# A hybrid attention and delta-rule backbone on one core: the order planner of TensorE puts dense products between small matmuls

## The chip, the cores and the metric

The kernel runs on one core of a Trainium2 chip. The metric is the device time of one execution in microseconds (us). PE is TensorE's matmul part, PEld its weight load, DVE VectorE, ACT ScalarE, POOL GpSimd and SP the engine whose queue issues the DMA transfers.

## What is computed

Two layers over 512 latent tokens and 256 context tokens of width 1024, all in f32. Each layer projects the modulated, normalised tokens once, and splits the columns into three kinds of heads: gated DeltaNet in both directions (8 heads of 64), global attention (4 query heads, 2 key heads) and windowed attention (the same, with a sink). An output projection and an MLP with squared ReLU follow. Cut to what matters:

```python
def hybrid_layer(x, cx, ...):
    sh_a, sc_a, gt_a, sh_m, sc_m, gt_m = ada_mod(cond, w_mod, b_mod)
    ...
    a_qkv, a_z, a_beta, a_alpha, b_qkv, c_qkv = split_cols(modulate(x, g_attn, sh_a, sc_a) @ w_in)
    ...
    o_a, oc_a = gdn_mixer(...)          
    o_b, oc_b = global_gqa(q, k, v, qc, kc, vc)
    o_c, oc_c = window_gqa(q, k, v, qc, kc, vc, wa_sink)
    x = x + gt_a * (jnp.concatenate([o_a, o_b, o_c], axis=-1) @ w_out)
    x = x + gt_m * sq_relu_mlp(modulate(x, g_mlp, sh_m, sc_m), w_mlp_in, w_mlp_out)
```

The delta rule (`gated_delta_chunked`) runs in chunks of 64 tokens: a triangular system per chunk and head, and then a scan over the chunks, whose state goes from one chunk to the next. Context chunks come first, then latent ones.

## The kernel before

The kernel doesn't write its instructions in the order of the code. `Model.run` (line 1744) records every operation of both layers in a `Program` through `Program.add` (line 353): its engine, what it must wait for, a modelled duration (`cost`, line 389), and for PE a number `dense`: the share of the 128 rows of the array that the product uses, times 0.6 if its output has at most 64 columns (line 382). Then `Program.layout` (line 428) plans the whole kernel in one pass of a list scheduler and `issue` (line 639) writes the instructions out engine by engine in the planned order. On the chip each engine works through its own order and waits where an operand isn't there. All instructions are issued by line 683, so the profile names that line throughout, and groups are told apart by tile names.

Dense products (`dense` 1.0) are those of the projections and the MLP (`ps<-b,w`, `ps<-w,b`, `ps<-h,w`; each weight slice is loaded into `st` and split into two tiles `w`, high and low part, by ACT and DVE, and three products per tile pair make up an f32 product), attention's scores, transposes and value products (`ps<-a,a`, `ps<-r,a`, `ps<-cst,g`, `ps<-g,g` of 128 rows), and the modulation `ps<-sm,cs`, which streams the 512 KB slices of `w_mod` through two buffers `sm`. Small products are those of the delta rule: the key products (`key_products`, line 1443, 64 rows), the inverse of the triangular systems (`pre`, line 1530, 32 rows, tiles `s`) and the scan (`scan_step`, line 1629, 64 rows and 64 columns, tiles `u`, `v`, `kv`, `kaq`, results in `pu`). A scan step has three groups of products on its chain (`pw`, `px`, `pk`), 8 heads and directions each, with work of DVE or ACT between them, and one off the chain (`po`). In the trace one f32 product counts twice, so a group of 8 stands there as x16.

What sets the order: an operation's rank is the length of the longest chain of modelled work from it to the end (line 445). For every engine there is a heap `avail` of the operations whose inputs are there, best rank first. At each step the engine whose clock is earliest takes the top of its heap; if its tiles have no free slot it is parked, otherwise it is placed. PSUM has 5 slots `ps` and 3 slots `pu` (`KINDS`, line 36).

The planner also models TensorE's clock with constants of its own (`WINDOW`, `COLD`, `WARM`, lines 308 to 310): it adds up the planned PE time of a stretch weighted by `dense` (`work`), and sets a flag `warm` for the next stretch from the sum. While the flag is off, a matmul is planned to take twice its time. In the kernel before, this model changes only planned durations; the choice among ready products goes by rank alone.

The order of the program is: modulation of layer 0; input projections for the first half of the delta-rule heads, its key products, systems and scan; the second half; attention's projections; attention and scan together with the modulation of the next stages; output projection and MLP; and the same for layer 1, whose context output isn't needed.

Of the kernel before, what the change touches and what calls it, by code (L numbers as in the profile page):

```python
# [303 lines left out]
PE, ACT, DVE, POOL, SP = range(5)  # L304
# [3 lines left out]
WINDOW = 4096 / 1.2  # L308
COLD = 0.36
WARM = 0.66  # L310
TABLES = {AF.Exp: 0, AF.Tanh: 0, AF.Ln: 1}


class Program:
# [38 lines left out]
    def add(self, eng, name, args, kw):  # L353
# [30 lines left out]
        if eng == ACT:  # L384
            op.table = TABLES.get(args[2])
        self.ops.append(op)
# [41 lines left out]
    def layout(self):  # L428
        ops = self.ops
# [10 lines left out]
        for k, l in chains.items():  # L440
            n = KINDS[k][2] + KINDS[k][3] + max(KINDS[k][5:])
# [43 lines left out]
        clock, avail, future = [0.0] * 5, [[] for _ in range(5)], [[] for _ in range(5)]  # L485
        parked = {k: [] for k in KINDS}
        queues, front, order, table = 0.0, 0, [], 0
        warm, work, spill, window = False, 0.0, 0.0, 0
# [44 lines left out]
        while len(order) < len(ops):  # L533
            best = None
            for e in range(5):
                t = clock[e] if avail[e] else max(clock[e], future[e][0][0]) if future[e] else None
                if t is not None and (best is None or t < best[0]):
                    best = t, e
            if best is None and early:
                n = heapq.heappop(early)[1]  # L540
# [5 lines left out]
            t, e = best  # L546
            now = max(now, t)
            while future[e] and future[e][0][0] <= t:
                n = heapq.heappop(future[e])[1]
                heapq.heappush(avail[e], (-ops[n].rank, n))  # L550
            n = heapq.heappop(avail[e])[1]
            o = ops[n]
            if longest - o.rank > AHEAD[e] and n != front and n not in forced and any(
                    x.slot is None and x.kind in HOARD for x in o.tiles):
# [25 lines left out]
            if e == PE:  # L580

                w = int(t / WINDOW)
                while window < w:
                    warm = work > (COLD if warm else WARM) * WINDOW
                    work, window = spill, window + 1
# [3 lines left out]
                d = (end - t) * o.dense  # L589
                over = min(1.0, max(0.0, end - (w + 1) * WINDOW) / (end - t))  # L590
                work, spill = work + d * (1 - over), spill + d * over
# [36 lines left out]
            while early and (longest + early[0][0] <= AHEAD[ops[early[0][1]].eng] or early[0][1] == front):  # L628
                n = heapq.heappop(early)[1]
# [1192 lines left out]
```

## Time and profile before

| | |
|---|---|
| median of 3 runs | 2344.86 us (2334.07, 2344.86, 2356.42) |
| profiled execution | 2335.23 us |
| its span, first to last instruction | 2333.4 us |
| mean granted clock of TensorE | 0.929 |
| busy: PE, PEld, DVE, ACT, POOL | 2119.1, 1690.0, 1214.4, 878.4, 358.0 us |
| matmuls | 18584 |

The span is cut into 40 slices of 58 us in the page's second part; a digit is a busy share in tenths, and PEclk is the clock granted to TensorE in tenths of full speed. The stages are read from the names of the tiles in each stretch: 0 to 200 us the first modulation and projections, 200 to 709 the mixers of layer 0, 709 to 1340 its output projection and MLP, 1340 to 1909 projections and mixers of layer 1, 1909 to the end its output projection and MLP.

### The profile page before, as it was taken

To read this page: it belongs to the slowest core of one execution; us is meant where nothing else is said; L and a number is where in the kernel's file an instruction comes from. 1 tells how busy PE (TensorE), PEld (TensorE's weight loads), DVE (VectorE), ACT (ScalarE), POOL (GpSimd) and SP (SyncE) were. 2 spreads that over 40 slices of the span, in tenths; PEclk is the share of its full clock that TensorE was granted. 3 is DMA by queue.
4 is the path that set the end of the run, shared out by engine and by line. 5 is a ranking of instruction groups with operands and counts; after the bars stand their busy time and mean duration, and the time that the engine had idled before them with its cause. 6 is when DMAs were issued, how large, how long until landed. Compare 5 with 4: busy or idle time off the path is not lost.

```text
span 2333.4 us, 45381 instructions
## 1 busy us (share of the span) xinstructions
PE 2119.1 (91%) x18584; PEld 1690.0 (72%) x18584; DVE 1214.4 (52%) x2481; ACT 878.4 (38%) x1717; POOL 358.0 (15%) x392
## 2 busy tenths in 40 slices
PE   5899999679989899999999888989869988999999
PEld 2687788446657788888888767678636766878777
DVE  4668547765653632332333485757754655334333
ACT  4736325336432521312222363543425444222321
POOL 0133323432320000000000012244411310000000
PEclk9888899779998999999999997979769989999999
DMA  7267425894763121221221327466675532322322
GB/s 276 83 183 201 118 77 160 250 296 123 213 214 115 46 73 57 77 72 46 73 66 66 95 78 195 130 186 200 204 207 160 165 97 69 102 91 99 100 91 82
DMA packets 250224, 305.49 MB, mean 131 GB/s; under 512 B 97952, under 2 KB 172704, under 8 KB 250016
## 3 DMA queue, kind: packets, MB, share of 16 engines
q1 hardware_dynamic: 250016, 302.59, 43.0%
q8 instruction: 146, 2.39, 0.4%
q14 instruction: 62, 0.51, 0.1%
HBM read 246.32 MB, written 56.20 MB: 130 GB/s over the span
## 4 chain that ended last, share of the span: by engine, by line
PE 72%; DVE 9%; DMA 8%; ACT 4%; issue 3%; SPq 2%; POOL 2%; DVEq 0%; ACTq 0%; POOLq 0%
PE ps L683 65%; PE pu L683 7%; DVE g L683 3%; DMA sm<-w_mod 2%; SPq L683 2%; ACT g L683 2%; DVE t L683 2%; DVE u L683 2%; ACT L683 1%; DVE w L683 1%; POOL u L683 1%; DMA u<-kk 1%; DMA u<-xT 1%; DMA st<-w_qkv 1%; ACT u L683 1%
## 5 line engine op out<-in xcount | busy, mean ns | idle before, releaser
L683 PE MATMUL ps<-b,w 128*128 128x512 f32 (+1 forms) x3936 | 832.2, 363 | 22.4 <-ACT b L683 10.6
L683 PEld LDWEIGHTS ps<-b,w 128*128 128x128 f32 x3936 | 661.7, 193 | 151.9 <-ACT b L683 13.4
L683 PE MATMUL ps<-h,w 128*128 128x512 f32 (+1 forms) x2304 | 476.0, 356 | 1.9 <-DVE w L683 0.9
L683 PEld LDWEIGHTS ps<-h,w 128*128 128x128 f32 x2304 | 381.3, 188 | 70.7 <-DVE w L683 4.9
L683 ACT ACTIVATE w<-st 128x1024 fp32r<-128x1024 f32 x192 | 198.1, 1055 | 600.9 <-PE ps L683 598.9
L683 DVE TENSOR_TENSOR w<-st,w 128x1024 fp32r<-128x1024 f32 x192 | 234.7, 1250 | 245.0 <-PE ps L683 177.1
L683 ACT ACTIVATE g<-ps 128x512 f32<-128x512 f32 (+4 forms) x334 | 164.7, 514 | 267.9 <-PE ps L683 265.7
L683 DVE SCALAR_TENSOR_TENSOR x<-ps,mod,x 128x512 f32<-128x512 f32 (+1 forms) x120 | 77.3, 659 | 276.7 <-PE ps L683 276.6
L683 PE MATMUL ps<-w,b 128*128 128x256 f32 x1536 | 214.0, 292 | 1.1 <-ACT g L683 0.7
L683 PEld LDWEIGHTS ps<-w,b 128*128 128x128 f32 x1536 | 196.3, 195 | 5.8 <-ACT g L683 1.1
L683 PE MATMUL ps<-sm,cs 128*32 128x256 f32 x688 | 88.6, 465 | 42.0 <-DMA sm<-w_mod 36.3
L683 DVE TENSOR_TENSOR g<-g 128x512 f32<-128x512 f32 (+3 forms) x112 | 57.9, 542 | 125.5 <-ACT h L683 118.9
L683 DVE SCALAR_TENSOR_TENSOR g<-ps,par,g 128x510 f32<-128x510 f32 (+3 forms) x176 | 104.0, 620 | 31.9 <-ACT g L683 31.3
L683 PE MATMUL ps<-cst,g 128*128 128x128 f32 (+1 forms) x502 | 95.7, 307 | 21.2 <-ACT g L683 16.4
L683 POOL MEMSET iv<- 96x64 f32 (+1 forms) x12 | 5.5, 454 | 675.1 <-DVE g L683 657.9
L683 ACT ACTIVATE g<-ps,t 128x256 f32<-128x256 f32 (+2 forms) x144 | 75.2, 529 | 75.8 <-DVE t L683 70.5
L683 PEld LDWEIGHTS ps<-cst,g 128*128 128x128 f32 (+1 forms) x502 | 60.9, 152 | 50.4 <-ACT g L683 28.5
L683 PE MATMUL ps<-g,g 128*64 128x128 f32 (+1 forms) x1056 | 92.1, 294 | 5.7 <-DVE g L683 3.7
L683 DVE TENSOR_REDUCE t<-ps 128x2 f32<-128x512 f32 (+3 forms) x104 | 62.8, 623 | 60.9 <-PE ps L683 58.3
L683 PE MATMUL pu<-u,kaq 64*64 64x64 f32 (+1 forms) x1344 | 90.5, 248 | 2.6 <-DVE u L683 1.7
L683 DVE TENSOR_TENSOR g<-g,g 128x512 f32<-128x512 f32 (+3 forms) x129 | 76.6, 627 | 28.6 <-ACT g L683 24.2
L683 PEld LDWEIGHTS pu<-u,kaq 64*64 64x64 f32 (+1 forms) x1344 | 66.9, 152 | 25.8 <-issue 9.5
(131 smaller groups left out, 2326.8 us busy)
## 6 DMA issues: line engine op xcount, KB each, us to landing
st<-w SPq DMA_DIRECT2D x128, 512.0 KB
sm<-w_mod SPq DMA_DIRECT2D x86, 512.0 KB
st<-w_qkv SPq DMA_DIRECT2D x24, 512.0 KB
st<-w_tm SPq DMA_DIRECT2D x24, 512.0 KB
kv<-kv SPq DMA_DIRECT2D x96, 128.0 KB
u<-gd SPq DMA_DIRECT2D x88, 128.0 KB
u<-kk SPq DMA_DIRECT2D x88, 128.0 KB
kaq<-kq SPq DMA_DIRECT2D x80, 128.0 KB
```

Source lines behind the costliest of these rows:

```text
L683: getattr(engines[o.eng], o.name)(*[real(x) for x in o.args], **{k: real(x) for k, x in o.kw.items()})
```

## The change

Where PE takes the top of its heap and this product isn't dense (`dense` under 0.9) while others are ready, the planner looks at its own running stretch: `into` is the time since the stretch began, `work` the weighted PE time so far. If a new stretch is about to begin, or `work` is under 0.5 of `into` (0.8 while the modelled clock is low), the best-ranked ready product with `dense` of at least 0.9 is taken and the small one goes back on the heap. Nothing else is edited; no operation is added, removed or altered.

```diff
 WARM = 0.66
+
+KEEP_WARM, GET_WARM, FULL = 0.5, 0.8, 0.9
...
             n = heapq.heappop(avail[e])[1]
+            if e == PE and ops[n].dense < FULL and avail[e]:
+
+                into = t - window * WINDOW
+                if t >= (window + 1) * WINDOW or work < (KEEP_WARM if warm else GET_WARM) * into:
+                    d = [x for x in avail[e] if ops[x[1]].dense >= FULL]
+                    if d:
+                        d = min(d)
+                        avail[e].remove(d)
+                        heapq.heapify(avail[e])
+                        heapq.heappush(avail[e], (-ops[n].rank, n))
+                        n = d[1]
             o = ops[n]
```

## Rows read from the trace of the kernel before

**Rows 1.** The page's second part: PE's busy tenths and its granted clock, 40 slices.

```profile
PE   5899999679989899999999888989869988999999
...
PEclk9888899779998999999999997979769989999999
```

**Rows 2.** Stages: stretch, length, busy us of each engine (instructions), PEclk, DMA share, GB/s.

```profile
196.00:440.00 244.00, 219.41 (x2937) 188.19 (x2935) 153.29 (x308) 103.81 (x201) 80.29 (x79) 0.90 0.49 140
440.00:540.00 100.00, 74.21 (x582) 45.07 (x582) 61.27 (x185) 40.55 (x112) 32.58 (x30) 0.76 0.95 278
540.00:709.00 169.00, 148.58 (x2666) 102.22 (x2660) 94.01 (x311) 76.09 (x224) 43.77 (x51) 0.95 0.62 187
709.00:1340.00 631.00, 616.45 (x3469) 534.00 (x3469) 240.14 (x369) 176.46 (x282) 0.00 (x0) 0.99 0.21 69
...
1480.00:1660.00 180.00, 166.09 (x2372) 142.21 (x2371) 119.09 (x227) 75.44 (x148) 73.85 (x69) 0.90 0.65 181
1660.00:1760.00 100.00, 70.62 (x798) 45.76 (x798) 57.46 (x153) 32.49 (x77) 26.80 (x24) 0.66 0.73 219
```

**Rows 3.** The page's fourth part: shares by engine of the chain that ended last.

```profile
PE 72%; DVE 9%; DMA 8%; ACT 4%; issue 3%; SPq 2%; POOL 2%; DVEq 0%; ACTq 0%; POOLq 0%
```

**Rows 4.** Short stretches, columns as in rows 2; engines in the order PE, PEld, DVE, ACT, POOL.

```profile
120.00:130.00 10.00, 9.54 (x145) 9.24 (x142) 0.69 (x1) 5.49 (x14) 0.00 (x0) 0.50 0.62 165
...
219.00:253.00 34.00, 30.69 (x453) 24.53 (x450) 15.23 (x27) 14.65 (x29) 16.50 (x18) 0.50 0.67 180
253.00:287.00 34.00, 34.00 (x402) 26.89 (x402) 17.43 (x37) 11.40 (x23) 5.96 (x5) 1.00 0.32 101
...
1400.00:1410.00 10.00, 7.78 (x145) 7.00 (x146) 2.14 (x4) 8.00 (x22) 0.00 (x0) 0.50 0.65 179
...
1526.30:1529.70 3.40, 3.40 (x56) 2.98 (x60) 0.84 (x2) 0.39 (x1) 3.20 (x3) 0.50 0.79 240
1536.50:1550.20 13.70, 12.05 (x159) 10.11 (x159) 7.55 (x14) 5.71 (x14) 9.43 (x9) 0.50 0.64 183
```

**Rows 5.** PE's timeline: start us, length us, products (count), idle before and its releaser.

```profile
246.72 1.12 PE L683 MATMUL pu<-v,u 64*64 64x64 f32 x16 [1.90 <-DVE v L683]
247.77 1.22 PE L683 MATMUL ps<-b,w 128*128 128x512 f32 x2
...
661.07 0.68 PE L683 MATMUL pu<-v,u 64*64 64x64 f32 x16
```

**Rows 6.** Timelines of ACT and DVE: weight tiles converted, before and after two stretches.

```profile
218.93 1.22 DVE L683 TENSOR_TENSOR w<-st,w 128x1024 fp32r<-128x1024 f32 x1
...
276.92 1.06 ACT L683 ACTIVATE w<-st 128x1024 fp32r<-128x1024 f32 x1 [0.36 <-PE ps L683]
...
1486.23 1.23 DVE L683 TENSOR_TENSOR w<-st,w 128x1024 fp32r<-128x1024 f32 x1 [0.93 <-ACT w L683]
...
1566.08 1.06 ACT L683 ACTIVATE w<-st 128x1024 fp32r<-128x1024 f32 x1 [2.74 <-PE ps L683]
```

**Rows 7.** PE's groups by form, 540 to 690 us: count, busy us, mean ns, idle before.

```profile
L683 PE MATMUL ps<-cst,g 128*128 128x128 f32 x136 | 24.2, 288 | 1.5 <-ACT g L683 1.2
...
L683 PE MATMUL pu<-v,u 64*64 64x64 f32 x176 | 8.0, 225 | 0.7 <-DVE v L683 0.7
```

**Rows 8.** The chain in order of time, end of layer 0's mixers: start us, us, what.

```profile
686.06 0.70 PE pu L683 x16
...
689.69 4.84 DMA sm<-w_mod
...
709.58 10.61 PE ps L683 x36
```

**Rows 9.** Waits of the whole span: who waited for whom, us in total, times, longest.

```profile
PE ps L683 <- DMA sm<-w_mod: 36.3, 21, 4.9
```

**Rows 10.** PE's timeline around 1750 us, columns as in rows 5.

```profile
1749.86 0.64 PE L683 MATMUL ps<-sm,cs 128*32 128x256 f32 x8 [1.98 <-DMA sm<-w_mod]
1750.43 0.70 PE L683 MATMUL pu<-s,s 32*32 32x32 f32 x58
```

## The prediction

> **What bounds the kernel now.** I read the busy slices of the page first. PE is nearly full almost everywhere [rows 1], and the chain that ended last lies on PE for 72% of the span [rows 3]. So PE is the bound, and its own speed is read from the line below it: the granted clock is 9 or 10 tenths in most slices and 6 to 8 in a few [rows 1]. The mean clock of the run is 0.929, and the records know two levels, 0.50 (1.2 GHz) and 1.00 (2.4 GHz); 2333.4 us x (1 - 0.929) x 2 = 331 us of the span ran at the lower level.
>
> Then I cut the span into stages [rows 2]. The MLP stage shown has clock 0.99 and PE busy 616 of 631 us; layer 1's is like it, and no small matmul runs in either, so the change can't touch them. What is at stake are the mixer stages, in which 64- and 32-row products of the delta rule stand between dense products. Three kinds of loss lie there. In 196 to 440 and 1480 to 1660 PE is about 90% busy with a clock of 0.90. In 440 to 540 PE is busy for only 74 of 100 us with the DMA engines at 0.95: PE waits for transfers. In 540 to 709 the clock is 0.95.
>
> Cutting finer, by the two clock levels [rows 4], shows where order could matter. From 219 to 253 us PE is busy for 30.69 of 34 us and the clock is 0.50 throughout; it did almost only small products. In the next 34 us, with dense products between, PE is busy for all 34 and the clock is 1.00. In the timeline the small groups run until dense products come at 247.8 [rows 5]. The dense products weren't missing: three weight tiles were converted by 220 us and the next conversion starts only at 276.9 [rows 6], so their products lay ready while small ones were issued. The second layer shows the same: weights converted by 1487, the next at 1566 [rows 6], and between them 13.7 us at 0.50 and three stretches of 3.4 us [rows 4].
>
> The Trainium skill, "TensorE: Matmul & The Clock Gate", section "What's actually happening", says that the clock is set by how busy PE has been recently. By that rule a PE that is 90% busy with small products would come back to full clock alone, the mix would be worth nothing, and the sum below would have only its cost, 4 us. The trace doesn't agree: 30.69 of 34 us busy at 0.50 [rows 4]. I go by the rows.
>
> **The change part by part.** No operation is added or removed; each engine gets the same instructions. Only PE's choice differs: where the best-ranked ready product is small and the planner's running share of dense work is under its bound, the best-ranked ready dense product goes first. Every engine's order and every transfer then follows from a new plan, which adds scatter that no row gives.
>
> *A, layer 0, 219 to 253.* A group of 16 products of 64 rows takes 1.12 us at 0.50 and 0.68 us at 1.00 [rows 5], so a busy microsecond falls to 0.61. 30.69 x 0.39 = 12.0 us.
>
> *B, layer 1.* 13.7 us with 12.05 busy, and three stretches of 3.4 us, each 3.40 busy [rows 4]: 22.25 x 0.39 = 8.7 us.
>
> *D, the key products at 120 to 130 and 1400 to 1410.* 9.54 + 7.78 us busy at 0.50 [rows 4], small too, but there the clock was down when they began. 17.3 x 0.39 = 6.8 us if dense products bring it back at once, 0 if none is ready. Half: 3.4 us.
>
> *C, 440 to 540.* Clock 0.76, so 48 us at the low level. With PE busy for 74 of the 100, an upper end is 48 x 0.74 x 0.45 = 16 us; the lower end is 0, as the transfers set the pace (0.95 of the DMA engines [rows 2]). The row is nearer to 0, and I take 0.
>
> Of A + B + D = 24.1 us not all reaches the end. Behind A, PE is full, so the time is handed on; but it runs into the transfer-bound 440 to 540 us, which swallows it unless the loads of w_mod start earlier too. I pass on half of layer 0's 12.0 + 1.7, which is 6.9. Layer 1's stage is followed by one that isn't as tight (DMA engines at 0.73, 1660 to 1760 [rows 2]); I pass on three quarters of 8.7 + 1.7, which is 7.8. Together 14.7 us; the ends are 0 and 24.1 (with C 40).
>
> *E, the cost.* A dense product put ahead of a small one delays the scan, which is a chain. From 540 to 690 one form of it has 176 products, 11 groups of 16 [rows 7], one per scan step. A step has three groups on its chain; with a second layer alike that makes 66. A dense product there takes 24.2 us / 136 = 0.18 us [rows 7]. All 66 hit and nothing to hide it: 66 x 0.18 = 11.9 us; none hit: 0. Attention's products fill PE beside the scan for most of this, which hides the delay; it is bare at the end, where scan groups and then loads of w_mod are last [rows 8]. I take a third, 4 us. The same cost hits the earlier stages, but there other dense work is queued behind it.
>
> What the change may also give: the products that read w_mod count as dense. Pulled into gaps they free their two load buffers sooner, and the loads that stand last before 709 us [rows 8] would come earlier. From 689.7 to 709.6 that is at most 20 us; I count none of it, as the last scan group at 686 [rows 8] stays late.
>
> Sum: -14.7 + 4 = -10.7 us. Against the profiled execution, 2335.23 us (span 2333.4), that is 2324.5. The median of the runs, 2344.86, lies 9.6 us above that execution; so the forecast is 2334 us, 0.5% less. A measurement of this kernel tells about 1% (23 us) from no change, its own three runs lying 22 us apart.
>
> **The rivals.**
>
> *The whole gain arrives.* A, B and D pass on in full and some of C as well: 24 to 40 us less, 2305 to 2321. For it: PE is the bound [rows 3], and it is full behind A [rows 4]. Against: the transfer-bound stage between.
>
> *Slower: the scan is starved.* Dense products are chosen by readiness in the plan, and where the plan's clock is thought low, one goes ahead of about every second small one. There are 44 scan steps with 3 groups, and 24 units whose inverse has 4: 132 + 96 = 228 groups. At 0.18 us each that is 41 us if nothing hides it; less some 10 us of gain, plus 31: 2376. It decides from about 33 us of bare delay (23 + 10), 183 groups. For it: the end of layer 0's mixer stage has the scan on the chain [rows 8]. A filler whose input is late costs more: PE waited 36.3 us in 21 waits for w_mod [rows 9], 1.7 each, and at 1749.9 a 1.98 us wait stands directly ahead of scan products [rows 10]. Against: from 540 on the clock is already 1.00 with attention mixed in, so the rule should seldom fire there.
>
> The Trainium skill, the same page, section "The mechanism", says matmuls start and end strictly in program order. The wait at 1749.9 agrees with it: the 58 small products behind begin after it [rows 10]. By this rule 20 such waits more, moved ahead of the scan, would make the sum 34 us worse.
>
> *It doesn't do what it says.* The planner's clock and times aren't the chip's: DVE and DMA arrive at other times, so the share that holds in the plan doesn't hold on PE, and the stretch from 219 falls as before. Or the clock doesn't answer to the mix at all. Then only E and scatter stay: 2345 + 4, within 10 us of no change. For it: PE idles 2 us in the cold stretch for an operand that the plan had expected earlier [rows 5].
>
> **How the numbers follow.** Forecast 0.36, whole gain 0.28, starved scan 0.19, no effect 0.17. Whole gain gives faster by over 1%; forecast and no effect lie within 1%: 0.53; starved scan gives slower. The range starts at the lower end of the whole gain and goes some way towards the starved scan: 2306 to 2371; the forecast's own is 2322 to 2347.
>
> **What would show it.** Right: no stretch of 10 us or more at clock 0.50 with PE 90% busy near 219 to 253 and 1537 to 1550; dense weight products between the small groups there; the mean clock up from 0.929 to 0.94 or more; the MLP stages unchanged in length. Right for E: the scan's last group before out_proj later against attention's last. Wrong: the same cold stretches with the same small groups (no effect), or a clock that rises while the mixer stages grow, with PE idle behind scan products or w_mod loads (starved). A time under 2321 with 440 to 540 shorter would say that I passed on too little.

## The result, and the profile after

The change makes the kernel slower: 2414.39 us (median of 4 runs, 2407.42 to 2429.47) against 2346.88 us of the kernel before beside it. The ratio is 1.03, 95% interval 1.023 to 1.037. The forecast was 2334 us, with a range up to 2371. The profiled execution took 2407.42 us with a span of 2405.6, 72.2 us longer than the span before.

The page of after, parts 1 and 2 (PE's line, its busy tenths and its clock):

```profile
PE 2211.4 (92%) x18584; PEld 1733.6 (72%) x18584; DVE 1210.7 (50%) x2481; ACT 879.4 (37%) x1719; POOL 357.2 (15%) x392
...
PE   5899999779999899999999898999869978999999
...
PEclk9999899679998999999999988758969979999999
```

PE's busy time rose from 2119.1 to 2211.4 us, by 92.3, for the same 18584 products. Its idle time fell, from 214.3 (2333.4 - 2119.1) to 194.2. So most of the loss isn't waiting: the same work takes PE longer. The clock line has a new dip, 7 5 8, in the 26th to 28th slices (1504 to 1684 us), and the mean clock is 0.919 where it was 0.929.

The stages of after, with the columns of [rows 2]; the last is the MLP stage:

```profile
196.00:440.00 244.00, 221.42 (x2824) 182.54 (x2822) 145.59 (x297) 94.86 (x188) 79.64 (x78) 0.90 0.49 138
440.00:540.00 100.00, 73.39 (x537) 44.27 (x536) 59.78 (x171) 33.15 (x97) 28.92 (x28) 0.68 0.85 251
540.00:731.00 191.00, 178.72 (x2781) 118.81 (x2780) 98.03 (x327) 85.35 (x246) 49.89 (x56) 0.95 0.59 175
...
1530.00:1620.00 90.00, 88.69 (x1018) 66.30 (x1014) 33.83 (x71) 23.80 (x55) 27.94 (x28) 0.54 0.38 111
...
731.00:1362.00 631.00, 616.46 (x3470) 533.79 (x3469) 240.44 (x370) 176.35 (x282) 0.00 (x0) 0.99 0.22 71
```

The MLP stage is the same to the digit (616.46 against 616.45 us busy in 631 [rows 2]). Layer 0's mixers end 22 us later; in 196 to 440 PE is 2.0 us busier for 113 products fewer. In layer 1, 90 us run at 0.54 with PE busy for 88.69 of them.

The chain in order of time, where the output projections begin (start us, length us, what):

```profile
731.83 69.04 PE ps L696 x383
...
1980.09 45.91 PE ps L696 x186
```

The second one in the kernel before:

```profile
1909.44 46.39 PE ps L683 x186
```

They began at 709.58 [rows 8] and 1909.44 before: 22.3 us are lost in layer 0 and 48.4 more (1980.09 - 731.83 against 1909.44 - 709.58) in layer 1's input and mixer stages. At the end of layer 1's mixers there is some waiting too. The scan's last groups stand there behind attention's last products, and of the last 20 us PE is busy for this much, at half clock:

```profile
1960.00:1980.00 20.00, 8.06 (x88) 6.41 (x88) 8.57 (x27) 3.74 (x9) 2.87 (x4) 0.50 0.10 27
```

Before it was 14.65 of the last 20 us (1889 to 1909), with attention's products still running beside the scan. So 6.6 us more are idle here, against 20 us less over the whole span.

The answers to [rows 4], and the cold stretch of layer 1:

```profile
120.00:130.00 10.00, 10.00 (x160) 6.82 (x160) 4.88 (x11) 4.87 (x14) 0.00 (x0) 1.00 0.50 127
219.00:253.00 34.00, 34.00 (x495) 23.00 (x495) 9.01 (x19) 9.64 (x23) 7.56 (x8) 0.82 0.41 113
253.00:287.00 34.00, 31.97 (x467) 25.94 (x456) 19.57 (x42) 10.97 (x23) 15.89 (x16) 0.88 0.46 137
1400.00:1410.00 10.00, 10.00 (x69) 8.91 (x68) 8.51 (x12) 9.90 (x14) 1.65 (x4) 1.00 0.57 168
...
1534.00:1616.00 82.00, 80.69 (x921) 60.17 (x918) 30.65 (x64) 20.92 (x48) 25.73 (x26) 0.50 0.38 114
```

Three of the four cold places did come up: 1.00 for 0.50 at 120 and at 1400, 0.82 for 0.50 at 219. But from 219 to 253 a PE that is now full at a higher clock gets 495 products done, against 453 in 30.69 busy us at 0.50 (not the same ones). And 1534 to 1616 is a new cold stretch, six times as long as the one of 13.7 us that stood there, with PE busy for 80.69 of 82 us.

PE's timeline of after (start us, length us, product, count), first at full clock, then inside the cold stretch:

```profile
1525.21 0.50 PE L696 MATMUL ps<-b,w 128*128 128x512 f32 x1
1525.63 0.45 PE L696 MATMUL pu<-u,kaq 64*64 64x64 f32 x8
1526.01 0.51 PE L696 MATMUL ps<-b,w 128*128 128x512 f32 x1
...
1556.48 0.58 PE L696 MATMUL ps<-b,w 128*128 128x256 f32 x1
1556.99 0.43 PE L696 MATMUL pu<-s,s 32*32 32x32 f32 x12
1557.35 0.58 PE L696 MATMUL ps<-b,w 128*128 128x256 f32 x1
```

This is the rule at work: one dense product, a handful of small ones, one dense product. It lies on PE without a gap. I counted the places in the order on PE where a small product follows a dense one, each a change to small and back: 319 before, 506 after (320 and 508 when they are counted in the traces by the products' shapes). Two theories came from this. **S**: every such change costs PE time of its own, which shows as busy. **C**: the mix, one product at a time, doesn't bring the clock back. There are two rivals. **T** is the prediction's starved scan: what is lost is PE waiting for a scan that comes late. **R**: any new plan of this kernel scatters by some per cent, and this one fell badly.

How the clock came to fall in layer 1 is a question that C doesn't answer. PE worked without a pause in the same mix while the clock was 1.00, and it fell near 1534 us:

```profile
1500.00:1530.00 30.00, 29.68 (x481) 19.12 (x479) 16.16 (x26) 20.29 (x31) 5.06 (x6) 1.00 0.64 153
...
1533.00:1536.00 3.00, 3.00 (x34) 2.09 (x32) 0.84 (x2) 0.38 (x1) 1.22 (x2) 0.68 0.42 103
```

### The profile page after: what moved, and what is told of

The parts are those of the page before. It is cut to its first block, busy times and chain, and to the rows that moved or that the text cites. A ratio compares the mean times of both kernels' runs of the same rounds, so it can differ in the third digit from the quotient of the medians.

```text
span 2405.6 us, 45367 instructions
## 1 busy us (share of the span) xinstructions
PE 2211.4 (92%) x18584; PEld 1733.6 (72%) x18584; DVE 1210.7 (50%) x2481; ACT 879.4 (37%) x1719; POOL 357.2 (15%) x392
## 4 chain that ended last, share of the span: by engine, by line
PE 63%; DVE 7%; DMA 3%; ACT 2%; issue 2%; SPq 1%; POOL 0%; ACTq 0%; DVEq 0%; POOLq 0%
PE ps L696 56%; PE pu L696 8%; DVE g L696 2%; DVE t L696 2%; SPq L696 1%; DVE u L696 1%; DMA sm<-w_mod 1%; ACT g L696 1%; DVE w L696 1%; DVE iv L696 0%; ACT u L696 0%; ACT L696 0%; ACT w L696 0%; DMA a<-qB 0%; DVE v L696 0%
## 5 line engine op out<-in xcount | busy, mean ns | idle before, releaser
L696 PE MATMUL ps<-b,w 128*128 128x512 f32 (+1 forms) x3936 | 869.5, 368 | 27.6 <-ACT b L696 10.6
L696 PE MATMUL ps<-w,b 128*128 128x256 f32 x1536 | 225.9, 299 | 2.6 <-DVE w L696 1.9
L696 PEld LDWEIGHTS ps<-w,b 128*128 128x128 f32 x1536 | 202.2, 199 | 9.2 <-DVE w L696 2.2
L696 PE MATMUL ps<-sm,cs 128*32 128x256 f32 x688 | 104.4, 464 | 36.3 <-DMA sm<-w_mod 30.3
L696 PE MATMUL pu<-u,kaq 64*64 64x64 f32 (+1 forms) x1344 | 99.8, 253 | 3.2 <-DVE u L696 2.4
L696 PE MATMUL ps<-g,g 128*64 128x128 f32 (+1 forms) x1056 | 98.3, 288 | 2.9 <-DVE g L696 2.6
L696 PEld LDWEIGHTS pu<-u,kaq 64*64 64x64 f32 (+1 forms) x1344 | 71.8, 154 | 33.5 <-issue 16.1
L696 DVE TENSOR_TENSOR g<-g,g 128x512 f32<-128x512 f32 (+3 forms) x129 | 74.7, 611 | 30.9 <-ACT g L696 25.6
```

The source lines that it names most:

```text
L696: getattr(engines[o.eng], o.name)(*[real(x) for x in o.args], **{k: real(x) for k, x in o.kw.items()})
```

## The experiments

**The price of a change alone.** A kernel with nothing but products on PE: 96 dense ones and 384 of 64 rows, in rounds of 1 dense and 4 small, of 8 and 32, and of 2 and 8.

```diff
+        for r in (1, 8, 2):
+            mix(r)            # 96 // r times: dense(r), small(4 * r)
+            dense(60)
+        for r in (1, 8):
+            small(512)
+            mix(r)
+            dense(60)
```

> Leaves out the whole computation: PE alone runs 96 dense products (128x128 by 512 columns) and 384 small ones (64x64 by 64, alternating row halves as in the scan) in each mix, 1 dense to 4 small, 8 to 32, 2 to 8, starting after dense work; then the mixes 1:4 and 8:32 again, each behind 512 small products; 60 dense products follow each mix. Theory S (each change between dense and small products costs PE time of its own, about 0.2 us on the way to small and 0.1 us back at full clock): a mix of 50 us of work (96 x 0.213 + 384 x 0.077) takes about 79 us as 1:4, 64 as 2:8 and 53 as 8:32. Rival N (no such cost, the extra PE time of the changed kernel is the clock's): 50 us in all three at full clock. Theory C (a mix holds the clock at the level at which it starts): the mixes behind dense work run at 1.00, the same mixes behind small products stay at 0.50 throughout, until the 60 dense products raise it. Rival: the mix raises the clock by itself within a few us.

Its timeline (an f32 product of 64 rows counts twice):

```profile
32.49 0.45 PE L483 MATMUL pu<-g,g 64*64 64x64 f32 x8
32.86 0.51 PE L483 MATMUL ps<-w,w 128*128 128x512 f32 x1
33.30 0.45 PE L483 MATMUL pu<-g,g 64*64 64x64 f32 x8
...
125.45 2.08 PE L483 MATMUL pu<-g,g 64*64 64x64 f32 x64
127.46 2.11 PE L483 MATMUL ps<-w,w 128*128 128x512 f32 x8
129.51 0.68 PE L483 MATMUL pu<-g,g 64*64 64x64 f32 x16
...
186.33 0.68 PE L483 MATMUL pu<-g,g 64*64 64x64 f32 x16
187.61 0.68 PE L483 MATMUL pu<-g,g 64*64 64x64 f32 x16
```

A round of 1 and 4 takes 0.81 us (33.30 - 32.49), eight of them 6.5; one round of 8 and 32 takes 4.06 (129.51 - 125.45). The same products, seven changes fewer, 2.44 us less: **0.35 us for a change to small and back**. Rounds of 2 and 8 give the same: 4 x 1.28 - 4.06 = 1.06 for three. The clock was 1.00 in all of it, so this is S without C. The 512 products of 64 rows ahead of the last two mixes didn't lower it, against what was expected of them, so this kernel says nothing on a clock that has fallen. In the dense product's row there is nothing to see but its 0.51 us, where 16 behind one another take 3.79, 0.24 each; the loss counts as busy.

**What the price belongs to, and the clock behind an idle stretch.** The second kernel of products alone puts dense products against f32 products of the full array (`square`) and against 32-row ones (`tiny`), then `square` against 64-row ones, in rounds of 1 and of 8. Its second part lets PE idle for some 18 us before each block.

```diff
+        for args in ((square, 1), (tiny, 8), (small, 4, square)):
+            for r in (1, 8):
+                mix(48, r, *args)
+                dense(60)
+        for seg in (lambda: mix(96, 1, small, 4), lambda: mix(96, 8, small, 4), lambda: small(512),
+                    lambda: tiny(2048), lambda: mix(96, 1, tiny, 6, narrow), lambda: mix(96, 8, tiny, 6, narrow)):
+            idle()
+            seg()
+            dense(60)
```

> Leaves out the whole computation. First part, after dense work: mixes in rounds of 1 and of 8, each 48 dense products and (a) 48 f32 products of the full 128x128 array, (b) 384 products of 32 rows; (c) 48 f32 products of the full array and 192 of 64 rows. If the price of a change comes with the size of the array that is used, (b) and (c) cost more as 1 than as 8 and (a) costs the same; if it comes with the kind of f32 product, (a) and (b) cost more and (c) the same. Second part, each behind an idle PE of some 13 us, so that the clock is at 0.50 when it begins, and each followed by 60 dense products: 1 dense to 4 of 64 rows; 8 to 32; 512 of 64 rows alone; 2048 of 32 rows alone; 1 dense of 256 columns to 6 of 32 rows, and 8 to 48. Theory C (a thin mix full of changes holds the clock down): 1 to 4 and 1 to 6 stay at 0.50 to their end, and the same products as 8 to 32 or 8 to 48 rise to 1.00 within some us. Rival: all rise, or none does before the 60 dense products.

```profile
43.77 0.48 PE L483 MATMUL ps<-w,w 128*128 128x512 f32 x1
44.08 0.38 PE L483 MATMUL pu<-g,g 128*128 128x128 f32 x2
44.22 0.48 PE L483 MATMUL ps<-w,w 128*128 128x512 f32 x1
...
80.56 1.95 PE L483 MATMUL pu<-g,g 128*128 128x128 f32 x16
...
84.17 1.95 PE L483 MATMUL pu<-g,g 128*128 128x128 f32 x16
...
118.17 0.50 PE L483 MATMUL ps<-w,w 128*128 128x512 f32 x1
118.61 0.33 PE L483 MATMUL pu<-g,g 32*32 32x32 f32 x16
118.86 0.50 PE L483 MATMUL ps<-w,w 128*128 128x512 f32 x1
...
151.69 1.29 PE L483 MATMUL pu<-g,g 32*32 32x32 f32 x128
154.94 1.24 PE L483 MATMUL pu<-g,g 32*32 32x32 f32 x107
```

Between two full-array products a change costs nothing: 0.45 us a round of 1 (44.22 - 43.77), 3.61 a round of 8. Against 32-row products it costs 8 x 0.69 - 3.25 = 2.27 us for seven, 0.32 each. The full-array f32 product against 64-row ones took 38.1 us in rounds of 1 (184.95 to 223.08) and 23.9 in rounds of 8 (236.81 to 260.67), 0.34 for each of 42 changes. So the price belongs to the part of the array that a product uses, not to its number format. The Trainium skill, "TensorEngine Tiling (Array Packing)", section "Key Properties", says that changing the tiling mode drains TensorE. These rows agree that such a change costs time, and give its size. They don't show what the time goes to. In the first kernel a weight load (PEld) behind a change starts together with its product, at 32.86 and at 33.30. In a run the loads are ahead: of the run from 127.46, three loads have begun by 127.81 and only two products:

```profile
32.86 0.19 PEld L483 LDWEIGHTS ps<-w,w 128*128 128x128 f32 x1
33.30 0.13 PEld L483 LDWEIGHTS pu<-g,g 64*64 64x64 f32 x1 [0.25 <-issue]
...
127.46 0.53 PEld L483 LDWEIGHTS ps<-w,w 128*128 128x128 f32 x3
127.46 0.73 PE L483 MATMUL ps<-w,w 128*128 128x512 f32 x2
```

The two loads behind a change take 0.19 and 0.13 us, 0.32 together. Whether the price is a drain, or these loads that no product hides, stays open. Nor does any run price a change to products that use all 128 rows and only 64 or 32 columns (`pu<-u,kaq` 128*64, `ps<-sm,cs` 128*32), which the kernel has too.

The second part, by stretches (columns as in [rows 2]):

```profile
292.00:421.00 129.00, 128.81 (x858) 75.92 (x858) 0.00 (x0) 0.13 (x1) 0.00 (x0) 0.50 0.00 1
425.00:442.00 17.00, 12.01 (x53) 9.59 (x52) 0.00 (x0) 4.67 (x8) 0.00 (x0) 0.99 0.00 0
459.00:504.00 45.00, 45.00 (x812) 37.45 (x810) 0.00 (x0) 0.00 (x0) 0.00 (x0) 1.00 0.01 3
541.00:569.00 28.00, 28.00 (x964) 27.94 (x959) 0.00 (x0) 0.00 (x0) 0.00 (x0) 1.00 0.02 4
601.00:715.00 114.00, 61.58 (x4081) 57.19 (x4084) 0.00 (x0) 0.00 (x0) 0.00 (x0) 0.50 0.02 4
749.00:831.00 82.00, 82.00 (x1237) 54.73 (x1235) 0.00 (x0) 0.00 (x0) 0.00 (x0) 0.50 0.01 2
869.00:915.00 46.00, 37.51 (x1201) 32.18 (x1199) 0.00 (x0) 0.60 (x1) 0.00 (x0) 1.00 0.02 7
```

This is C by itself. The block in rounds of 1 and 4 starts at 292 at half clock and stays there for 129 us, PE busy throughout; the clock rises only in the dense products behind it (425). The same products in rounds of 8 and 32 are at 1.00 from 459. The 32-row mix repeats it: rounds of 1 at 0.50 for 82 us, rounds of 8 at 1.00. In the first kernel the 1 and 4 mix kept a clock of 1.00 that it found; here it didn't bring back one that had fallen. 64-row products alone did (541 to 569); 32-row ones alone, with PE busy for 61.58 of 114 us, did not. Why layer 1's mix lost a clock of 1.00 near 1534 us, where the first kernel's mix kept it, no run shows.

**Longer runs.** The rule of the change, but once it fires PE takes dense products for 1 us of planned time (then 2 us).

```diff
                 if t >= (window + 1) * WINDOW or work < (KEEP_WARM if warm else GET_WARM) * into:
+                    fill = t + 1000
+                if t < fill:
                     d = [x for x in avail[e] if ops[x[1]].dense >= FULL]
```

> The rule fires as in the change, but then stays with dense products for 1 us of planned time, so that PE changes from dense to small 361 times instead of 506 (319 before). Theory S: 42 changes more than before at 0.3 us, 13 us, less what the clock gains: 2335 to 2365, PE busy 2110 to 2140. Theory C (the thin mix holds the clock low): the long stretch at 0.50 in layer 1 is gone, mean clock 0.93 or more; the time follows the clock only, about 2385. Theory T (the scan is starved): a burst of 1 us delays a scan product more than one product of 0.2 us does, so the time is 2414 or more, with idle PE at the end of both mixer stages.

> As e1 with dense runs of 2 us: 329 changes against 361. Theory S: 11 us less than e1, about 2312. Theory T: a burst of 2 us holds the scan up more, above 2323.

1 us: 2323.3 us, ratio 0.988 (0.984 to 0.993); 361 changes, clock 0.936. 2 us (`fill = t + 2000`): 2311.75 us, ratio 0.986 (0.982 to 0.990); 329 changes, clock 0.938. Both are faster than the kernel before, by 1.2 and 1.4%. At S's price alone runs of 1 us would have been 15 us slower than it; the gain comes with a clock of 0.933 to 0.942 in its four runs, against 0.914 to 0.927 in the 13 of the kernel before beside them. T wanted 2414 us or more for runs of 1 us, and runs of 2 us slower than those; neither came. Two windows of the 1 us kernel answer the cold stretches directly:

```profile
219.00:253.00 34.00, 33.62 (x700) 27.93 (x701) 12.65 (x30) 11.60 (x31) 10.79 (x13) 1.00 0.66 179
...
1530.00:1620.00 90.00, 84.86 (x1110) 74.50 (x1110) 64.87 (x124) 34.58 (x68) 43.95 (x39) 0.94 0.70 202
```

From 219 to 253 the clock is 1.00 and PE does 700 products, where the change did 495 and the kernel before 453. From 1530 to 1620 it is 0.94 instead of 0.54.

**More of the rule.** The dense share wanted is raised to 0.8, or set to 0.5, at either level of the modelled clock.

```diff
-KEEP_WARM, GET_WARM, FULL = 0.5, 0.8, 0.9
+KEEP_WARM, GET_WARM, FULL = 0.8, 0.8, 0.9
```

> Both shares 0.8: the rule fires more often, 1041 changes from dense to small against 506 in the change and 319 before. Theory S: 722 more than before at 0.3 us, some 215 us: 2520 to 2600, PE busy over 2300. Theory C alone: the mix is denser, the clock rises to 0.94 or more, and the time is below the change's 2414. Theory T: later scans, 2420 to 2460, with more idle PE at the ends of the mixer stages and PE busy unchanged at 2211 or less.

> The change with both shares 0.5, so that the planner's low clock asks for no more dense products than its high one: 531 changes. Theory S: 25 more than in the change, 9 us more: 2410 to 2435. Rival (the share of 0.8, used while the planner thinks the clock low, does the harm): 2350 to 2380.

0.8 and 0.8: 2858.05 us, ratio 1.217 (1.212 to 1.221), with 1041 changes. 0.5 and 0.5: 2442.09 us, ratio 1.042 (1.036 to 1.048), with 531 changes, a little over what S had for it; so the 0.8 of the change isn't what hurts. The first is far over the bound that the price of a change alone gave, and one of its stretches shows why:

```profile
1800.00:2100.00 300.00, 298.97 (x1690) 201.01 (x1687) 59.76 (x141) 44.81 (x95) 50.15 (x48) 0.51 0.23 66
```

A rule written to hold the clock up leaves it at 0.51 for 300 us, with PE busy for 298.97 of them.

**A new plan without any rule.** The kernel before, with 3 ns more in the planner's cost of a DVE operation.

```diff
-            return 69 + 1.042 * n + (61 if len(ins) > 2 else 0), 0
+            return 72 + 1.042 * n + (61 if len(ins) > 2 else 0), 0
```

> The kernel before with one modelled duration altered (DVE 3 ns longer per instruction), without the rule: a new plan with 308 changes against 319. Theory S: 11 fewer at 0.3 us, 3 us: 2335 to 2355. Rival R (any new plan of this planner scatters by some per cent, and the 3% of the change are such scatter): 2370 or more, or 2320 or less.

2349.37 us, ratio 1.001 (0.999 to 1.004). R falls as far as one new plan can show it: a loss of 3% isn't scatter of this size.

**Fewer changes, no rule for the clock.** The kernel before; PE stays with the kind of product that it is at (dense or small) while the best of that kind gives away less than 10 us of rank.

```diff
+SLACK = 10000
...
             n = heapq.heappop(avail[e])[1]
+            if e == PE and avail[e] and (ops[n].dense < 0.9) != small:
+                d = [x for x in avail[e] if (ops[x[1]].dense < 0.9) == small and ops[n].rank + x[0] < SLACK]
+                if d:
...
```

> The kernel before without the rule; instead PE stays with the kind (dense or small) that it has as long as the best product of the other kind is ahead by less than 10 us of rank: 258 changes from dense to small against 319 before. Theory S: 61 fewer at 0.35 us, 21 us less: 2315 to 2335. Theory C: without a rule for the clock the small products bunch, the clock falls oftener than before, 2350 or more. Theory T (order by rank is what the scan needs): scan products wait for dense ones, 2360 or more.

2326.5 us, ratio 0.990 (0.984 to 0.996), 258 changes. Fewer changes pay without any rule for the clock. They aren't shown to pay without its help: the clock was 0.923 to 0.927 in the four runs, against 0.908 to 0.925 in the seven of the kernel before beside them, medians 0.925 and 0.917. At S's price 61 changes are 21 us of the 24.8, and the clock could have given nearly as much. Its profiled execution was its slowest, 2332.65 us, so the split below shows little of the gain.

**Where the loss sits.** The change's rule for products of the input stages alone (`phase % 3 == 0`), then for those of the attention stages alone (`== 1`).

```diff
-            if e == PE and ops[n].dense < FULL and avail[e]:
+            if e == PE and ops[n].phase % 3 == 0 and ops[n].dense < FULL and avail[e]:
```

> The rule as in the change, but only for products of the two stages up to attention's projections (461 changes). Theory S and C: most of the loss lies here, where the 82 us at 0.50 of layer 1 are: 142 changes more than before at 0.35 us plus the clock: 2390 to 2415. Theory T (the scan late at the ends of the mixers): about as before, 2340 to 2360.

> The rule only for products of the stages with attention and the second scan (373 changes). Theory S: 54 changes more at 0.35 us, 19 us: 2355 to 2375. Theory T: the loss of the change lies here, 2385 to 2415, with idle PE ahead of the output projections.

Inputs alone: 2417.11 us, ratio 1.028 (1.022 to 1.035), 461 changes: the whole loss. Attention alone: 2378.05 us, ratio 1.013 (1.006 to 1.020), 373 changes, 27 us where S gave 19. T had it the other way, with the loss in the attention stages and none in the inputs. The two don't add up to the change's 67 us; each makes a plan of its own.

**Both cures together.** Runs of 1 us, and outside of them PE stays with its kind, with 10 and with 20 us of slack.

```diff
+            if e == PE and avail[e] and t >= fill and (ops[n].dense < FULL) != small:
+                d = [x for x in avail[e] if (ops[x[1]].dense < FULL) == small and ops[n].rank + x[0] < SLACK]
...
```

> The rule with dense runs of 1 us of planned time (as in e1), and between them PE stays with its kind up to 10 us of rank (as in e4): 287 changes. Theory S with C: below both e1 (2323) and e4 (2327) if the two gains add: 73 changes fewer than in e1 at 0.35 us, 2295 to 2315. Rival: both gains are the same one, or the scan now waits: 2320 to 2340.

> As e7, with 20 us of rank: 265 changes. Theory S: 22 fewer than e7, 8 us less. Theory T: by now the scan's order suffers, more than e7.

2309.07 us, ratio 0.985 (0.982 to 0.989), and 2305.97 us, ratio 0.986 (0.980 to 0.992). They beat both kernels. The three at 0.985 to 0.986 (these two and runs of 2 us) can't be told apart, and their intervals overlap with that of runs of 1 us.

**The two prices against all runs.** Change in PE's busy time against the kernel before, from two terms: 0.35 us for each change more, and half of the time more at 0.50, which is 2 x (1 - clock) x span (331 us before). An estimate, since the price is that of full clock, and a cold stretch in which PE idles costs less than half. The profiled execution of the kernel before also had a high clock, 0.929: its 27 runs beside the experiments lie at 0.908 to 0.927. So the clock's share of a loss tends to come out large, and that of a gain small.

| kernel | changes | clock | changes x 0.35 | half of cold time | sum | PE busy, measured |
|---|---|---|---|---|---|---|
| after | 506 | 0.919 | +65 | +29 | +95 | +92 |
| runs of 1 us | 361 | 0.936 | +15 | -17 | -2 | 0 |
| runs of 2 us | 329 | 0.938 | +4 | -22 | -19 | -23 |
| share 0.8 | 1041 | 0.824 | +253 | +336 | +589 | +533 |
| share 0.5 | 531 | 0.911 | +74 | +51 | +125 | +117 |
| new plan | 308 | 0.915 | -4 | +34 | +30 | +13 |
| fewer | 258 | 0.923 | -21 | +14 | -7 | +8 |
| inputs alone | 461 | 0.905 | +50 | +63 | +113 | +96 |
| attention alone | 373 | 0.931 | +19 | -2 | +17 | +30 |
| runs and fewer | 287 | 0.928 | -11 | 0 | -11 | -23 |
| the same, 20 us | 265 | 0.940 | -19 | -28 | -47 | -35 |

The change's own row closes within 3 us: 65 us from changes, 29 from the clock, less 20 us of idle time. Elsewhere the sum misses by up to 17 us, and by 56 of 533 for the share of 0.8: good for what is large here, not for single per cents.

## Why the prediction was wrong, by its steps

- **What bounds the kernel** held. PE is the bound, the MLP stages didn't move, and what PE lost came through to the end.
- **E failed.** It priced a dense product ahead of a small one as a delay of the chain behind it, 0.18 us from the group's busy time, mostly hidden because PE is full. It measured 0.35 us of PE's own time for every change, and a full PE hides none of it: there it goes straight to the end. 187 changes more make 65 us where the step had 4. The sentence under it, that no operation is added and each engine gets the same instructions, let me take PE's work as fixed; its order is part of its work. That dense products with small ones between don't take the time of dense ones in a row, no step asked.
- **A and B failed in layer 1 and half held in layer 0.** The price of a warm small product (0.61 of a cold one) leaves out the changes that come with a lone dense product every few small ones. 219 to 253 came to 0.82, not 1.00, and lost to changes what it got from the clock. Layer 1's 13.7 us became 82 us at 0.50. In the rows before, dense products came at 247.8 and the next 34 us were at 1.00 [rows 4, 5]: I read that as dense work between small work. In the runs it mattered how long the dense work stays together. With runs of 1 us that stretch is at 1.00, as A had it.
- **D held**: 1.00 for 0.50 at both places. **C** gave nothing, as taken: PE is busy for 73.39 us of the 100 where it was 74.21, at a clock even lower, 0.68 for 0.76.
- **The starved scan** had the sign and little of the mechanism. It wanted idle time behind the scan and w_mod. PE's wait for w_mod fell, from 36.3 us [rows 9]. The wait of PE's `pu` products for tiles `u`, which DVE writes, rose from 21.1 us to 30.9, and of this rise 7.3 us lie in the last 30 us of layer 1's mixers (9.8 against 2.5). There the scan's last group did come later against attention's last, which was the sign for E; but that is some 7 us of the 72:

```profile
PE pu L696 <- DVE u L696: 30.9, 17, 7.5
PE ps L696 <- DMA sm<-w_mod: 30.3, 19, 4.9
```

- **No effect** fell too: the order did change as planned, one dense product at a time.
- The clock rule that I set aside, of the Trainium skill's "TensorE: Matmul & The Clock Gate", section "What's actually happening", fares no better behind the result than ahead of it: 300 us at 0.51 with PE busy for 298.97. What PE shows as busy includes the time lost at changes. That this lost time is also what holds the clock down is my reading, not shown.

## What to carry to other kernels

Order on PE has a price: count how often products on the full array and products on a part of it take turns, and price each turn from a small kernel before interleaving them. If dense work is to keep the clock up, give it in runs (1 or 2 us of planned time did it here), not one product at a time. When PE's busy time rises for the same products, look at their order and at the clock before looking for waits.

## What was unexpected of the hardware

A change between full-array and 64- or 32-row products cost 0.32 to 0.35 us at full clock, one between two kinds of full-array product nothing, and none of it shows as idle time. At half clock, a PE busy for 128.81 of 129 us stayed there throughout with 1 dense product to 4 small ones, and was at full clock with the same products in groups of 8 and 32. 64-row products alone held 1.00 too, though the planner weighs them as if they did little for the clock.
